# A hybrid trunk layer on one core: w_mod loads over all blocks of stage one, split low words in its last block, and blocks of 2, 3, 4, 4, 4 tiles in stage two

## The chip, the cores and the metric

The kernel runs on one core of one Trainium2 chip. The metric is the time of one execution on the device in microseconds, the median of several runs. The engines are named as in the profile: PE (TensorE matmul) and PEld (its weight loads), DVE (VectorE), ACT (ScalarE), POOL (GpSimd), SP (SyncE, which only issues DMAs here).

## The reference

One streaming step of one layer. The prompt is 2048 tokens of width 1024, and there are 8 samples of 16 tokens, with their own conditioning vectors, state and caches. All in float32:

```python
sh1, sc1, g1, sh2, sc2, g2 = split(silu(c) @ w_mod + b_mod, 6)      # w_mod 1024 x 6144
h = rmsnorm(x, norm1_g) * (1 + sc1) + sh1
proj = h @ w_in                                                     # 1024 x 3592
o_a = gated_delta(conv_silu(proj[q,k,v of A]), gate, beta, g)       # 4 heads x 128, state over time
o_b = band_attention(rmsnorm(q_b), rmsnorm(k_b), v_b, rel_bias)     # 8 heads x 64, own chunk of 64 and 8 before
x = x + g1 * (concat(o_a, o_b) @ w_out)
h = rmsnorm(x, norm2_g) * (1 + sc2) + sh2
x = x + g2 * (relu(h @ w_up) ** 2 @ w_down)                         # 1024 x 4096 x 1024
```

The outputs are y of prompt and samples, and the new convolution rows, delta states, and band keys and values.

## The kernel before

Tokens are cut into tiles of 128: tiles 0 to 15 are the prompt, tile 16 (SMP) holds the eight samples. To keep float32 precision every operand of a large product is a high word plus a low word, and each product is three matmuls (high x high, high x low, low x high; `mm3`, and lines 518 to 520 and 1477 to 1479).

`weights` brings one weight tile of 128 x 1024 words: the raw floats by DMA (line 174), the high word by a ScalarE copy (line 175), and the low word in one of two ways. The first time it is the difference raw minus high on GpSimd (line 82, called from line 180), and for chosen matrices it is stored to DRAM (line 183); later blocks load the stored word by DMA (line 178). w_in's low words are stored in the first block of stage one, those of w_out and w_down in the first block of stage two, those of w_up in its second. There are 3 buffers for raw and 4 for the split pair.

Stage one (`phase1`) goes over the blocks of tiles in BLOCKS1. Each block has a first projection (`proj_a`: gates, then 12 column tiles of q, k and v of the delta rule, `psq`, then gates again) and a second (`proj_b`: q, k and v of the attention, 12 weight tiles, `psb`). The second projections of the fifth and the third block (LATE, which counts from 0) come at the end, behind that of the last block. The last block has two tiles. The delta rule of a block runs as a generator beside the projections of the next one, and the attention of the first block of stage two beside the last three second projections.

w_mod has 48 pieces of 512 x 256. The 16 for sh1 and sc1 are loaded at the start; the other 32 wait in `mod_todo`. After each column tile of `proj_a` in a later block `mod_step` issues one (line 281, into a buffer of the tag x, of which there are three, shared with the rows of x), and two ticks later `mod_chunk` multiplies it, adds it to a row, and after each second piece finishes 256 columns of one section.

Stage two (`phase2`) goes over BLOCKS2. For each block it runs `out_proj` (`pso`) and then `ffn`: 32 columns of w_up (`psu`), and after each four of them two halves of w_down for each tile (`psd`). The attention of the *next* block is queued as a generator and its steps are spread over this `ffn` by `pace`, (8 + 1) steps for each tile and 4 more; where the next block holds SMP, the attention of the samples (`sample_gen`, 74 steps) follows in the same queue. A unit of attention is one head and one tile: scores (`psS`), softmax, transposes of the probabilities (`psP`), values (`pv`, line 1283, one matmul for each key tile: t + 1 for tile t, at most five). The `out_proj` of a block needs all units of its tiles. In the first block of stage two all low words are made on GpSimd, in the second those of w_up. When a block has four tiles, the first column of w_up is run in two parts of 256 tokens.

The order of the instructions on each engine is set when the program is built, by a scheduler with a timeline of its own; it can place an instruction of the next step ahead of one of the present step.

Of the kernel before, what the change touches and what calls it, by code (L numbers as in the profile page):

```python
# [8 lines left out]
F32 = mybir.dt.float32  # L9
# [5 lines left out]
P = 128  # L15
# [4 lines left out]
SMP = 16  # L20
# [10 lines left out]
EPS = 1e-6  # L31
NEG = -1.0e30
BLOCKS1 = [[0, 1, SMP], [2, 3, 4], [5, 6, 7], [8, 9, 10], [11, 12, 13], [14, 15]]
BLOCKS2 = [[0, 1], [2, 3, 4, 5], [6, 7, 8, 9], [10, 11, 12, 13], [14, 15, SMP]]
NGRP = 4
NT2 = max(len(b) for b in BLOCKS2)
LATE = (4, 2)
# [14 lines left out]
class Trunk:  # L52
# [113 lines left out]
    def weights(self, name, k0, c0, a, b):  # L166

        nc = self.nc
        n = a * b
        w = self.wp.tile([P, 2, 1056], F32R, tag="w", name="w", bufs=self.nw)  # L170
        v = lambda k: w[:, k, 0:n].rearrange("p (a b) -> p a b", a=a)
        src = self.i[name][0][k0 * P:(k0 + a) * P, c0:c0 + b].rearrange("(k p) c -> p k c", p=P)
        r = self.wp.tile([P, 1056], F32, tag="raw", name="raw", bufs=self.nraw)[:, 0:n]
        nc.sync.dma_start(r.rearrange("p (a b) -> p a b", a=a), src)
        nc.scalar.copy(w[:, 0, 0:n], r)  # L175
        key, kept = (name, k0, c0), self.s_w[name]
        if key in self.stored:
            nc.sync.dma_start(w.bitcast(F32)[:, 1, 0:n], kept[self.stored[key]][:, 0:n])
            return v(0), v(1)
        self.tt(w[:, 1, 0:n], r, w[:, 0, 0:n].bitcast(F32), ALU.subtract, eng=nc.gpsimd)  # L180
        if self.keep[name]:
            m = sum(k[0] == name for k in self.stored)
            nc.sync.dma_start(kept[m][:, 0:n], w.bitcast(F32)[:, 1, 0:n])
            self.stored[key] = m
        return v(0), v(1)
# [282 lines left out]
    def proj_a(self, tiles, hT, nxt=()):  # L468

        nc = self.nc  # L470
        n = len(tiles)
        T = n * P
        smp = SMP in tiles
        Tp = T - (P if smp else 0)
        blk = {}
        blk["kq"] = []
        ssq = self.bp.tile([P, self.nt, AH], F32, tag="ssq", name="ssq", bufs=2)
        ssk = self.bp.tile([P, self.nt, AH], F32, tag="ssk", name="ssk", bufs=2)
        ba = self.bp.tile([P, self.nt, 8], F32, tag="ba", name="ba", bufs=2)

        def gates(half):

            xs = [] if half else [self.normed(None, t) for t in nxt]
            m = 256 + 8 * half
            ws = self.wslices("w_in", 0, GA0 + 256 * half, m, KT, 4)
            for j, tl in enumerate(tiles):
                tmps = self.load_a(nxt[j], xs[j], 0, 1) if j < len(xs) else None
                ps = self.gp.tile([P, 512], F32, tag="g", name="psg")
                for k in range(KT):
                    wh, wl = ws[k]  # L490
                    self.mm3(ps[:, 0:m], hT[:, k, 0, j * P:(j + 1) * P], hT[:, k, 1, j * P:(j + 1) * P], wh, wl,
                             k == 0, k == KT - 1)
                th = self.cp.tile([P, 256], F32, tag="th", name="th", bufs=1)
                sg = self.cp.tile([P, 256], F32, tag="sgw", name="sgw", bufs=2)
                self.act(th, ps[:, 0:256], AF.Tanh, scale=0.5)
                self.stt(sg, th, 1.0, ps[:, 0:256], ALU.add, ALU.mult)
                if half:
                    nc.scalar.copy(ba[:, j], ps[:, 256:264])  # L498
                nc.sync.dma_start(self.s_sg[tl][:, half * 256:(half + 1) * 256], sg)
                self.tick(24 * 256)  # L500
                if tmps:
                    self.load_b(j, tmps)
            for j in range(len(tiles), len(xs)):
                self.load_b(j, self.load_a(nxt[j], xs[j], 0, 1))

        gates(1)
        for h in range(AH):
            kq = self.bp.tile([P, 2, self.nt * P], F32, tag="kq", name="kq", bufs=8)
            blk["kq"].append(kq)
            for sec in (1, 0, 2):  # L510
                c = sec * 4 + h
                ws = self.wslices("w_in", 0, c * P, P, KT, KT)
                ps = self.gp.tile([P, 512], F32, tag="g", name="psq")
                pc = ps[:, 4:4 + T]
                for k in range(KT):
                    wh, wl = ws[k]
                    mm = nc.tensor.matmul
                    mm(pc, wh, hT[:, k, 0, 0:T], start=(k == 0), stop=False)  # L518
                    mm(pc, wh, hT[:, k, 1, 0:T], start=False, stop=False)  # L519
                    mm(pc, wl, hT[:, k, 0, 0:T], start=False, stop=(k == KT - 1))  # L520
                self.tick(24 * T)
                dst = kq[:, 1 - sec] if sec < 2 else self.cp.tile([P, self.nt * P], F32, tag="vT", name="vT", bufs=2)
                y = self.cp.tile([P, self.nt * P], F32, tag="y", name="y", bufs=2)
                if Tp:
                    nc.scalar.copy(ps[:, 1:4], self.hist[:, c])
                    self.conv(y[:, 0:Tp], ps[:, 1:4 + Tp], c, Tp)
                    nc.scalar.copy(self.hist[:, c], ps[:, Tp + 1:Tp + 4])
                if smp:
                    pres = self.cp.tile([P, NB, 3 + SL], F32, tag="pres", name="pres", bufs=2)
                    hs = self.hists[:, c].rearrange("p (b w) -> p b w", w=3)  # L530
                    pv = pc[:, Tp:T].rearrange("p (b s) -> p b s", s=SL)
                    nc.scalar.copy(pres[:, :, 0:3], hs)
                    nc.scalar.copy(pres[:, :, 3:], pv)
                    nc.scalar.copy(hs, pv[:, :, SL - 3:])
                    self.conv(y[:, Tp:T].rearrange("p (b s) -> p b s", s=SL), pres, c, P, sub=True)
                self.act(ps[:, 0:T], y[:, 0:T], AF.Tanh)
                self.stt(dst[:, 0:T], ps[:, 0:T], 1.0, y[:, 0:T], ALU.add, ALU.mult)
                self.later(lambda c=c, dst=dst: self.qkv_out(c, dst, tiles, ssq, ssk))
                if self.bi:
                    self.mod_step()  # L540
        self.flush()
        gates(0)
        blk.update(ssq=ssq, ssk=ssk, ba=ba)
        return blk
# [481 lines left out]
    def phase1(self):  # L1026
        nc, tc = self.nc, self.tc
        with ExitStack() as st:
# [25 lines left out]
            last = len(B) - 1  # L1054
            self.load_hT(B[0], xs, 0, 1)
            for bi, tiles in enumerate(B):
                self.bi = bi
                self.keep["w_in"] = bi == 0
                if bi == 1:
                    self.rel_bias()  # L1060
                self.drain_to(bi - 2)
                blk = self.proj_a(tiles, self.hT, B[bi + 1] if bi in LATE else ())
                if bi == last:
                    break
                self.gdn(blk, tiles, bi)
                self.pace(0.95 * (cb(bi) * (bi not in LATE) + ca(bi + 1)), 6000)
                if bi not in LATE:
                    self.proj_b(tiles, self.hT, B[bi + 1])
# [3 lines left out]
            self.ap = R_("p1at")  # L1072
            self.queue(self.attention_first(BLOCKS2[0]), 1 + BH + BH // 2 * len(BLOCKS2[0]) + BH + 2, lane=2)
            self.queue(self.conv_gen(), 6, lane=1)
            self.gdn(blk, tiles, last)
            rest = [last] + list(LATE)
            self.pace(0.85 * sum(cb(b) for b in rest))
            for b, nb in zip(rest, rest[1:] + [None]):
                self.proj_b(B[b], self.hT, B[nb] if nb is not None else ())
            self.drain()  # L1080
            nc.sync.dma_start(self.o["gdn_prompt"][0, 0].rearrange("h k v -> k h v"), self.S)
# [242 lines left out]
    def sample_gen(self):  # L1324
# [7 lines left out]
        nc.sync.dma_start(bias, self.s_bs.rearrange("h s c -> (h s) c"))  # L1332
        nats = []
        for src in (self.s_q[SMP], self.s_kn):
            nat = self.sp.tile([P, 512], F32, tag="kn", name="nat", bufs=2)
            nc.sync.dma_start(nat, src)
            nats.append(nat)
        nc.vector.memset(qb, 0.0)
# [14 lines left out]
        for b in range(NB):  # L1353
# [4 lines left out]
            for t in range(4):  # L1358
                if t == 2:
                    yield  # L1360
                kn = self.sp.tile([P, 4, P], F32, tag="kn", name="kn", bufs=2)
# [163 lines left out]
    def phase2(self):  # L1525
        nc, tc = self.nc, self.tc
        with ExitStack() as st:
# [4 lines left out]
            self.hT = self.p2.tile([P, KT, 2, self.nt * P], F32R, name="hT2")  # L1532
            for bi, tiles in enumerate(BLOCKS2):
                n = len(tiles)
# [12 lines left out]
    def run(self):  # L1547
        self.nraw, self.nw = 3, 4
        self.deferred, self.lanes, self.pending, self.fill_rate, self.fill_acc = [], ([], [], []), [0, 0, 0], 0.0, 0.0
        self.front, self.solved, self.spent = 0, 0, 0  # L1550
        self.constants()
        self.phase1()
        self.phase2()
# [35 lines left out]
```

## Time and profile before

| | |
|---|---|
| median of 3 runs | 3214.93 us (3213.71 to 3215.14) |
| profiled execution | 3219.78 us |
| its span, first to last instruction | 3217.7 us |
| granted clock, mean | 0.975 |
| PE busy | 3072.2 us (95%) |
| DVE, ACT, POOL busy | 1765.4, 1471.7, 574.9 us |
| bytes moved by DMA | 751.62 MB |
| stage one ends, stage two begins | at about 1118 us |

A row of windows gives a stretch (start:end in us from the span's start), its length, then for PE, PEld, DVE, ACT and POOL the busy time and in brackets the number of instructions, then the granted TensorE clock as a share of full speed, the busy share of the 16 DMA engines, and GB/s. A row of waits gives who waited for whom, the total in us, how often, and the longest. A row of a group of instructions gives line, engine, operation, result and operands, shapes and count, then busy time and mean ns of one, then the idle time of the engine before them.

### The profile page before, as it was taken

How to read it: one execution, taken by the hardware profiler on the slowest of the kernel's cores; microseconds unless marked ns; L12 is line 12 of the kernel's file. 1: busy time of each engine (PE TensorE's matmuls, PEld its weight loads, DVE VectorE, ACT ScalarE, POOL GpSimd, SP SyncE). 2: the span in 40 equal slices, each digit the busy share in tenths (PEclk: the TensorE clock that was granted, in tenths of full speed). 3: DMA queues.
4: the chain of work that ended last, by engine and by line, in shares of the span. 5: the costliest groups of instructions: out<-in, count | busy, mean ns of one | idle time of the engine just before them, and what ended most of it. 6: DMA issues, size and time to landing. Idle time of an engine off the chain costs nothing.

```text
span 3217.7 us, 52979 instructions
## 1 busy us (share of the span) xinstructions
PE 3072.2 (95%) x19577; PEld 2720.7 (85%) x19577; DVE 1765.4 (55%) x4358; ACT 1471.7 (46%) x2803; POOL 574.9 (18%) x487
## 2 busy tenths in 40 slices
PE   6999999999989979988999999999999999998998
PEld 5998988899988978878888888888888887787997
DVE  4775777777868663777225556244556433243223
ACT  3554544555656555654334435344434433333332
POOL 3631212120212337631122110000000000000000
PEclk9999999999989989989999999999999999999999
DMA  9799897887978768885565666566675666677776
GB/s 295 232 291 292 255 295 222 258 263 240 298 244 272 227 224 265 253 289 159 177 200 182 211 232 213 179 191 200 196 258 176 213 226 225 221 245 227 255 247 196
DMA packets 630267, 751.62 MB, mean 234 GB/s; under 512 B 59808, under 2 KB 483728, under 8 KB 627960
## 3 DMA queue, kind: packets, MB, share of 16 engines
q1 hardware_dynamic: 624248, 716.78, 70.1%
q0 software_dynamic: 5760, 31.46, 2.9%
q8 instruction: 154, 2.52, 0.3%
q14 instruction: 105, 0.86, 0.1%
HBM read 635.48 MB, written 115.52 MB: 233 GB/s over the span
## 4 chain that ended last, share of the span: by engine, by line
PE 74%; DMA 14%; DVE 7%; ACT 2%; issue 2%; SPq 1%; POOL 1%; ACTq 0%; DVEq 0%; POOLq 0%
PE psu L1477 8%; PE psu L1478 7%; PE psu L1479 7%; PE psd L164 7%; PE psd L162 7%; PE psd L163 7%; PE psq L518 2%; PE psq L519 2%; PE psq L520 2%; PE psb L163 2%; PE psb L162 2%; PE psb L164 2%; PE pv L1283 2%; DMA x<-in_x_prompt_dram 2%; PE psS L1265 2%
## 5 line engine op out<-in xcount | busy, mean ns | idle before, releaser
L175 ACT CAST w<-raw 128x1024 fp32r<-128x1024 f32 (+1 forms) x528 | 551.8, 1047 | 359.2 <-PE psd L164 170.5
L1477 PE MATMUL psu<-hT,w 128*128 128x512 f32 (+2 forms) x1304 | 469.0, 361 | 4.2 <-ACT hT L104 4.2
L1478 PE MATMUL psu<-hT,w 128*128 128x512 f32 (+2 forms) x1304 | 468.3, 359 | 0.1
L1479 PE MATMUL psu<-hT,w 128*128 128x512 f32 (+2 forms) x1304 | 465.9, 357 | 0.3 <-POOL w L82 0.3
L162 PE MATMUL psd<-w,u 128*128 128x512 f32 x1088 | 431.0, 396 | 1.3 <-DVE u L82 0.8
L164 PE MATMUL psd<-w,u 128*128 128x512 f32 x1088 | 429.4, 396 | 0.0
L163 PE MATMUL psd<-w,u 128*128 128x512 f32 x1088 | 426.4, 392 | 0.0
L82 POOL TENSOR_TENSOR w<-raw,w 128x1024 fp32r<-128x1024 f32 (+1 forms) x132 | 320.1, 2434 | 325.0 <-ACT w L175 242.2
L79 DVE SCALAR_TENSOR_TENSOR psu<-psu,r 128x512 f32<-128x512 f32 (+2 forms) x160 | 98.9, 618 | 421.5 <-ACT r L92 421.4
L82 DVE TENSOR_TENSOR y<-y,psd 128x512 f32<-128x512 f32 x238 | 162.5, 685 | 246.2 <-PE psd L164 245.2
L1477 PEld LDWEIGHTS psu<-hT,w 128*128 128x128 f32 x1304 | 246.4, 189 | 38.1 <-ACT hT L104 4.9
L1479 PEld LDWEIGHTS psu<-hT,w 128*128 128x128 f32 x1304 | 246.4, 189 | 33.9 <-POOL w L82 0.9
L1478 PEld LDWEIGHTS psu<-hT,w 128*128 128x128 f32 x1304 | 246.5, 189 | 31.4 <-DVE hT L82 0.8
L92 ACT ACTIVATE r<-psu 128x512 f32<-128x512 f32 (+2 forms) x160 | 85.5, 534 | 380.0 <-issue 216.8
L164 PEld LDWEIGHTS psd<-w,u 128*128 128x128 f32 x1088 | 204.1, 188 | 46.5 <-DVE u L82 0.2
L163 PEld LDWEIGHTS psd<-w,u 128*128 128x128 f32 x1088 | 204.6, 188 | 45.6 <-issue 1.9
L162 PEld LDWEIGHTS psd<-w,u 128*128 128x128 f32 x1088 | 204.4, 188 | 44.6 <-DVE u L82 1.0
L162 PE MATMUL psb<-w,hT 128*128 128x256 f32 x816 | 237.5, 292 | 0.5 <-ACT hT L104 0.5
L163 PE MATMUL psb<-w,hT 128*128 128x256 f32 x816 | 235.4, 289 | 2.7 <-DMA w<-s_w_in 2.5
L164 PE MATMUL psb<-w,hT 128*128 128x256 f32 x816 | 235.1, 289 | 1.3 <-DVE hT L82 1.1
L518 PE MATMUL psq<-hT,w 128*128 128x384 f32 (+1 forms) x576 | 196.3, 341 | 8.3 <-ACT ba L498 8.2
L519 PE MATMUL psq<-hT,w 128*128 128x384 f32 (+1 forms) x576 | 194.7, 338 | 0.0
(316 smaller groups left out, 6501.2 us busy)
## 6 DMA issues: line engine op xcount, KB each, us to landing
raw<-in_w_up_dram SPq DMA_DIRECT2D x160, 512.0 KB
raw<-in_w_down_dram SPq DMA_DIRECT2D x160, 512.0 KB
raw<-in_w_in_dram SPq DMA_DIRECT2D x156, 512.0 KB
w<-s_w_in SPq DMA_DIRECT2D x130, 512.0 KB
w<-s_w_down SPq DMA_DIRECT2D x128, 512.0 KB
w<-s_w_up SPq DMA_DIRECT2D x96, 512.0 KB
raw<-in_w_out_dram SPq DMA_DIRECT2D x40, 512.0 KB
x<-in_x_prompt_dram SPq DMA_DIRECT2D x38, 512.0 KB
```

Of the source, the lines that this page charges most:

```text
L79: (eng or self.nc.vector).scalar_tensor_tensor(out, in0, scalar, in1, op0, op1)
L82: (eng or self.nc.vector).tensor_tensor(out, in0, in1, op)
L92: self.nc.scalar.activation(out, in_, func, **kw)
L162: mm(out, lh, rh, start=first, stop=False)
L163: mm(out, lh, rl, start=False, stop=False)
L164: mm(out, ll, rh, start=False, stop=last)
L175: nc.scalar.copy(w[:, 0, 0:n], r)
L518: mm(pc, wh, hT[:, k, 0, 0:T], start=(k == 0), stop=False)
L519: mm(pc, wh, hT[:, k, 1, 0:T], start=False, stop=False)
L1477: mm(ps[:, c0:c1], wh, h2[:, k, 0, c0:c1], start=(k == 0), stop=False)
L1478: mm(ps[:, c0:c1], wh, h2[:, k, 1, c0:c1], start=False, stop=False)
L1479: mm(ps[:, c0:c1], wl, h2[:, k, 0, c0:c1], start=False, stop=(k == KT - 1))
```

## The change

- BLOCKS2 becomes 2, 3, 4, 4 and 4 tiles; SMP stays in the last block, which now has three prompt tiles beside it.
- A counter `slot` runs over the 60 column tiles of the five later blocks of stage one; a piece of w_mod is loaded after 32 of them, evenly, and no longer after each of the first 32.
- A flag `mix` is set during both projections of the last block of stage one. While it is set, every other call of `weights` makes the low word on GpSimd although a stored one exists. It isn't stored again.
- In `sample_gen` the two tiles `nat` take buffers of the tag htmp and no longer those of kn.

```diff
-BLOCKS2 = [[0, 1], [2, 3, 4, 5], [6, 7, 8, 9], [10, 11, 12, 13], [14, 15, SMP]]
+BLOCKS2 = [[0, 1], [2, 3, 4], [5, 6, 7, 8], [9, 10, 11, 12], [13, 14, 15, SMP]]
...
         key, kept = (name, k0, c0), self.s_w[name]
-        if key in self.stored:
+        self.turn += self.mix
+        if key in self.stored and not (self.mix and self.turn % 2):
             nc.sync.dma_start(w.bitcast(F32)[:, 1, 0:n], kept[self.stored[key]][:, 0:n])
             return v(0), v(1)
         self.tt(w[:, 1, 0:n], r, w[:, 0, 0:n].bitcast(F32), ALU.subtract, eng=nc.gpsimd)
-        if self.keep[name]:
+        if self.keep[name] and key not in self.stored:
...
                 self.later(lambda c=c, dst=dst: self.qkv_out(c, dst, tiles, ssq, ssk))
-                if self.bi:
+                self.slot += self.bi > 0
+                if self.bi and self.slot * 32 // 60 > (self.slot - 1) * 32 // 60:
                     self.mod_step()
...
                 self.drain_to(bi - 2)
+                self.mix = bi == last
                 blk = self.proj_a(tiles, self.hT, B[bi + 1] if bi in LATE else ())
...
             for b, nb in zip(rest, rest[1:] + [None]):
+                self.mix = b == last
                 self.proj_b(B[b], self.hT, B[nb] if nb is not None else ())
...
         for src in (self.s_q[SMP], self.s_kn):
-            nat = self.sp.tile([P, 512], F32, tag="kn", name="nat", bufs=2)
+            nat = self.hp.tile([P, 4, P], F32, tag="htmp", name="nat", bufs=2).rearrange("p a b -> p (a b)")
             nc.sync.dma_start(nat, src)
...
+        self.slot, self.mix, self.turn = 0, False, 0
```

## Rows read from the trace of the kernel before

**Rows 1.** Windows of stage two: out-projection and feed-forward of blocks 1, 2, 4, 5.

```profile
1118.20:1162.00 43.80, 34.93 (x230) 33.09 (x231) 23.67 (x45) 16.66 (x29) 17.89 (x12) 0.81 0.99 341
1162.00:1413.90 251.90, 234.74 (x1520) 211.17 (x1520) 166.08 (x337) 148.83 (x274) 156.80 (x85) 0.97 0.77 243
1413.90:1503.00 89.10, 74.97 (x541) 71.68 (x540) 63.26 (x151) 38.55 (x73) 10.70 (x13) 0.85 0.59 193
1503.00:1920.70 417.70, 412.34 (x1999) 343.30 (x1997) 189.10 (x373) 172.73 (x286) 77.93 (x52) 0.99 0.60 197
1920.70:1975.40 54.70, 51.51 (x436) 50.93 (x434) 36.46 (x85) 20.06 (x34) 1.94 (x3) 1.00 0.68 236
...
2451.40:2885.90 434.50, 428.92 (x2411) 346.44 (x2410) 166.15 (x368) 170.60 (x276) 4.83 (x14) 0.99 0.68 220
2885.90:2930.60 44.70, 38.85 (x299) 38.10 (x298) 20.12 (x44) 10.42 (x13) 1.39 (x2) 0.92 0.88 273
2930.60:3217.70 287.10, 272.86 (x1361) 246.43 (x1358) 81.89 (x133) 97.72 (x141) 0.55 (x1) 0.98 0.72 228
```

**Rows 2.** Waits of PE from 1118 to 1503 us.

```profile
PE psP L1273 <- DVE sS L87: 10.3, 5, 5.6
...
PE psu L1479 <- POOL w L82: 0.3, 2, 0.2
```

**Rows 3.** Value matmuls of the first two attentions: ns min/median/max, first and last start.

```profile
L1283 PE MATMUL pv<-PT,KV x136: 274/282/582, 1158.3 to 1431.6; 128*128 128x256 f32 x136
...
L1283 PE MATMUL pv<-PT,KV x160: 274/281/415, 1449.9 to 1906.1; 128*128 128x256 f32 x160
```

**Rows 4.** Groups of VectorE's instructions by shape, 1195 to 1414 us.

```profile
L82 DVE TENSOR_TENSOR of<-otmp 64x128 f32<-64x128 f32 x20 | 22.7, 1133 | 1.1 <-DMA s_ob<-of 0.9
...
L87 DVE TENSOR_SCALAR sS<-sS,sm 128x640 f32<-128x640 f32 x10 | 12.5, 1252 | 0.3
```

**Rows 5.** The same groups, 2000 to 2390 us.

```profile
L87 DVE TENSOR_SCALAR sS<-sS,sm 128x640 f32<-128x640 f32 x24 | 13.2, 552 | 0.7
...
L82 DVE TENSOR_TENSOR of<-otmp 64x128 f32<-64x128 f32 x28 | 7.8, 280 | 0.4
```

**Rows 6.** Windows of stage one, second to sixth block; last row: sixth block's `proj_b`.

```profile
205.00:299.00 94.00, 92.62 (x689) 82.58 (x687) 56.37 (x151) 47.13 (x110) 2.98 (x5) 0.98 0.95 296
299.00:389.00 90.00, 86.85 (x733) 83.79 (x732) 58.86 (x166) 45.82 (x96) 29.89 (x28) 0.98 0.82 259
389.00:473.00 84.00, 80.94 (x498) 71.54 (x497) 67.87 (x181) 38.14 (x88) 12.80 (x11) 0.98 1.00 308
473.00:531.00 58.00, 53.66 (x521) 47.63 (x521) 41.72 (x117) 28.17 (x66) 13.40 (x13) 0.94 0.67 204
531.00:604.00 73.00, 72.93 (x463) 64.42 (x462) 59.75 (x188) 35.30 (x80) 8.12 (x10) 1.00 0.89 270
...
708.00:778.00 70.00, 69.00 (x487) 65.44 (x486) 52.67 (x165) 40.77 (x96) 3.20 (x4) 1.00 0.91 271
...
808.00:872.00 64.00, 60.31 (x496) 58.73 (x495) 55.63 (x191) 39.09 (x100) 12.42 (x11) 1.00 0.93 298
872.00:945.00 73.00, 65.52 (x559) 60.98 (x558) 40.53 (x139) 39.62 (x87) 12.79 (x19) 0.85 0.94 300
```

**Rows 7.** Timeline of PE: two starts, six matmuls of 256 columns apart.

```profile
910.20 0.28 PE L162 MATMUL psb<-w,hT 128*128 128x256 f32 x1
...
910.91 0.28 PE L162 MATMUL psb<-w,hT 128*128 128x256 f32 x1
```

**Rows 8.** Waits of PE from 2886 us to the end.

```profile
PE psh L345 <- DVE xn L87: 8.3, 2, 4.7
```

**Rows 9.** Issues of the later w_mod loads: ns min/median/max, first and last start.

```profile
L281 SPq DMA_DIRECT2D rawx<-in_w_mod_dram x32: 368/384/1625, 202.0 to 587.3; - x32
```

**Rows 10.** Waits of PE from 389 to 531 us.

```profile
PE ptq L552 <- DVE kq L79: 3.1, 1, 3.1
```

**Rows 11.** GpSimd's split of a weight tile, 1162 to 1414 us.

```profile
L82 POOL TENSOR_TENSOR w<-raw,w 128x1024 fp32r<-128x1024 f32 x63 | 151.8, 2416 | 68.6 <-ACT w L175 46.3 <-PE psu L1479 11.9 <-DMA raw<-in_w_up_dram 6.4
```

**Rows 12.** Waits of GpSimd from 808 to 945 us.

```profile
POOL KV L1136 <- PE pv L1180: 23.2, 2, 16.9
```

## The prediction, made before the changed kernel was run

> **What bounds the kernel now.** I read the windows of stage two first [rows 1], cut where the out-projection of a block ends and its feed-forward part begins. TensorE is busy nearly all the time, so the question is only where it is not, or not at full clock. For each window I use one number, called its loss: its length less PE's busy time, plus (1 - granted clock) times its length, since a matmul takes twice as long at the lower level. Idle time at the low level is counted twice, so it is an upper bound. In order, the losses of stage two are 17.2 us (8.9 + 8.3) for the first block's out-projection, 24.7 for its feed-forward, 27.5 (14.1 + 13.4) for the second's out-projection, and then 9.5, 3.2, 9.9, 9.4 and 20.0 (this last with the tail, where the output is written). The first block and its hand-over hold 69.4 us; nothing later is like it.
>
> Why there? The waits of PE in that stretch are led by the transposes of the probabilities, which wait for VectorE's softmax [rows 2]. The first block's feed-forward, of two tiles, carries the attention of four. Its value matmuls run until 1431.6 us, 17.7 us after the feed-forward ended (1413.9); those of the next block end at 1906.1, 14.6 us before theirs does [rows 3]. From its first to its last unit (32 units of head and tile), the first attention took 273 us, 8.8 us for each of 31 steps. It was going flat out and still came late, and the out-projection behind it had to wait. VectorE's share there also grew in size: with GpSimd busy 157 of 252 us, the sum of the two halves of a unit's output takes 1133 ns and the 640-wide softmax scaling 1252 ns [rows 4]; with GpSimd nearly idle they take 280 and 552 [rows 5].
>
> In stage one [rows 6] the losses are 3.3, 5.0, 4.7 and 7.8 us from 205 to 531 us (20.8 together), near nothing until 808, then 3.7 and 18.4 (7.5 idle, the rest clock 0.85) for 872 to 945 us, the last block's second projection. There the DMA engines are busy 0.94 of the time.
>
> **Part by part.**
>
> *Blocks of 2, 3, 4, 4, 4 for 2, 4, 4, 4, 3.* The sizes are the same set, so matmuls of the projections, and loads of weights, keep their number. Attention moves: the first feed-forward carries tiles 2 to 4, 24 units for 32, the second 32 units over three tiles for 32 over four, the fourth three tiles and the sample for two and the sample. Each moved five-wide unit is 3200 matmul columns; at 0.118 us for 256 [rows 7] 1.48 us, eight of them 12 us, off one block and onto another: zero in the sum, if PE has them ready.
> First block: its feed-forward has 234.7 us of PE work, now 223. With the end of the out-projection and about 20 us of loss, 24 units have some 247 us, 10.3 us each, against the 8.8 that were reached. So the late end goes. The hand-over's 27.5 then falls to about the 9.4 of the last out-projection, which has three tiles and no late attention: -18. Of the 41.9 ahead of it I take another -4: one q load in four and a quarter of the softmaxes are gone (a quarter is 10.5), but the start of the attention remains. -22; bounds -8 (late end shortened only) and -32.
> Second block: three tiles of feed-forward are 273 us of PE (the last window of [rows 1]), 32 units 47, an out-projection 45: 365 us, 11.4 us for a unit. That lies above 8.8 and under the 14.7 that the second attention had (456 us for 31 steps [rows 3]), and GpSimd splits only w_up there (78 us busy). So it should keep up; denser work costs a little: +4, bounds 0 and +39 (the losses of the first block's feed-forward and hand-over, 52.2, in place of 9.5 and 3.2). DMA: the storing of w_up's low words goes along into the shorter block. 197 GB/s over 418 us are 82 MB; over 335 us that is 245 GB/s, what the first feed-forward moves now (243, at a share of 0.77 [rows 1]) with 0.3 us of waits of PE for a weight split there [rows 2]. Zero.
> Last block: at its start PE waits 8.3 us for VectorE's normalised rows [rows 8]; with four tiles the first weight column runs in two parts, so that the first half begins earlier. A three-tile block without this now stands second. Gain and loss cancel: 0, bounds 6 either way. The fourth block gets one more tile of attention beside the sample; its loss of 9.9 over 434 us says there is room. Zero.
>
> *w_mod loads spread.* 32 loads of 0.5 MB, now one after each of the 32 first column tiles of blocks two to four (12, 12, 8), all between 202 and 587 us [rows 9]. After: 6, 6, 7, 6, 7 over five blocks. So six of them, 3.1 MB, leave the second and the third block each, where DMA is busy 0.95 and 1.00; each takes its four small matmuls, its addition and its part of the row with it. But no row has PE wait for one: from 389 to 531 us the largest wait is for VectorE (3.1 us [rows 10]). Work moves and does not vanish; of 20.8 I take -3, bounds -10 and +4 (4 us is what three more x tiles, waiting for the shared buffers in the fifth block, could cost: that block's loss is now near 0).
>
> *Every other weight tile splits its low word in the last block.* 14 of 28 loads of 0.5 MB go, 8 in the first projection (which gets 7 w_mod loads, 3.7 MB against 4.2 saved: even), 6 in the second. There a weight tile feeds two tiles, 24 matmuls, 2.8 us, and wants 1.05 MB: 370 GB/s, where 300 are moved at a share of 0.94. That window is bound by DMA; 3.1 MB less at 300 GB/s are 10.5 us. In exchange, a split of 2.42 us on GpSimd [rows 11] behind ScalarE's copy, on an engine busy 13 of 73 us. Cover: four weight buffers, three tiles ahead, 8.5 us. -9; bounds -15 and +10.
> Against it speaks that two VectorE instructions grew by 0.85 and 0.70 us where GpSimd was busy with such splits [rows 4, 5]. VectorE is busy 40.5 of 73 us in this window [rows 6], which covers 14 times 0.85, 12 us, over the last block; without the cover it is rival (b). The Trainium skill (SBUF — State Buffer, Who interferes with whom) has a rule that goes further: GpSimd's ports are VectorE's second pair, and a VectorE instruction that needs this pair, for a second SBUF input or a two-port mode, is shut out for the whole of a GpSimd instruction. The trace agrees in direction, with means grown by 0.85 and 0.70 us. By the rule, 14 splits of 2.42 us could hold VectorE for 34 us, an estimate from that page and the split's row, and the sum would be +13 with all of it on the path.
>
> *The rest.* The sample's two q and k tiles take the buffers of the transposed input, free in mid feed-forward; hidden behind PE at 98.7% busy in that block [rows 1], and 2 us if not. The extra condition on storing is never reached with storing on. Zero.
>
> Sum: -22 + 4 + 0 - 3 - 9 = -30. The profiled execution took 3219.78 us (span 3217.7, 2.1 around it): 3189.8. The median of the runs, 3214.93, is 4.85 lower; on that footing 3185.
>
> **Rivals.**
> (a) The attention has a rate, not a number: a unit needs about what it is given wherever VectorE, ScalarE and PE alternate. Then block one keeps its losses but for 8 us, and block two, more densely packed than now, comes late: +39 in its feed-forward and the next out-projection. -8 + 39 - 3 - 9 = +19: 3234. For it: the late end, and that units took 14.7 us in the second block; against: these were paced, and 8.8 was reached. It decides if a unit takes more than 11.4 us there.
> (b) GpSimd holds the split words back. It works in order, and in the last block it stood 16.9 us before a K and V load that waited for value matmuls [rows 12]. A split behind that is late by 16.9 less 8.5 of cover, 8.4 us, with the low clock after it +10: 3204. It needs the split to stand behind the load in the order. In its other form the 12 us of lengthened VectorE instructions lie on the path and nothing is gained: -22 + 4 - 3 + 12 = -9, 3206.
> (c) The late end goes only in part and the start of the attention costs as before: -8 for -22: 3199.
> (d) The change doesn't do what it says for time: spread loads meet no wait, half the low words are off a queue that is then waited for by others, and what block one gains block two loses: 3215.
>
> **Chances.** Forecast 0.54; (a) 0.11; (b) 0.13; (c) 0.12; (d) 0.10. A measurement of this kernel can tell about 0.2%, 6.4 us. Faster: forecast, (b) and (c), 0.79; same: (d), 0.10; slower: (a), 0.11. The forecast's own range is 3165 to 3202. All good bounds at once would be 3152; I reach to 3155, and up past (d) to 3218, leaving out (a) and little more.
>
> **What would show it.** Right: the value matmuls of the first attention end before the first down projection does; the second out-projection at a clock above 0.95 and under 60 us; the window of the last block's second projection some 9 us shorter with DMA share down and 6 splits on GpSimd; losses of the second feed-forward under 15. Wrong: value matmuls after the end of the second feed-forward (a), PE waiting for a w that GpSimd wrote in the last block (b), an unchanged first feed-forward (c). What would make it wrong in size is mostly the start of the attention, in the first out-projection and just behind it, which I left almost as it is, and the order of the instructions, which is fixed when the program is built and can shift anywhere.

## The result

| kernel | median, us | runs | to the kernel before |
|---|---|---|---|
| before, in the same set | 3213.76 (3209.55 to 3215.14) | 5 | 1 |
| changed | 3192.74 (3188.05 to 3202.53) | 5 | 0.9928 [0.9907, 0.9949] |
| changed, second set | 3197.25 (3184.76 to 3206.42) | 7 | 0.9948 [0.9928, 0.9967] |

By the ratio on record the change makes the kernel faster by 0.72%, 23 us of 3214, where 30 were forecast; the two medians of the table lie 21 us apart. In the second set it is 0.52%, 17 us. Gains and losses in us below are worked out from the ratios where no profile is named. The profiled execution of the changed kernel was the longest of its five: 3202.53 us, span 3200.8.

Windows of stage two of the changed kernel, with the columns of [rows 1]: out-projection and feed-forward of blocks one and two, the out-projection of block three, and both of block five.

```profile
1126.30:1168.10 41.80, 34.54 (x241) 32.18 (x242) 24.62 (x57) 18.71 (x35) 16.51 (x13) 0.88 1.02 352
1168.10:1407.60 239.50, 222.04 (x1430) 199.62 (x1428) 143.83 (x288) 137.92 (x248) 160.32 (x87) 0.96 0.82 254
1407.60:1461.00 53.40, 48.14 (x398) 46.98 (x396) 42.09 (x104) 27.33 (x49) 6.51 (x7) 1.00 0.76 258
1461.00:1792.30 331.30, 322.42 (x1771) 295.02 (x1770) 174.16 (x352) 163.47 (x281) 79.24 (x53) 0.99 0.77 251
1792.30:1847.60 55.30, 54.93 (x464) 54.52 (x463) 39.33 (x96) 22.38 (x39) 2.52 (x5) 1.00 0.67 230
...
2774.30:2829.30 55.00, 51.01 (x402) 49.74 (x401) 32.23 (x68) 12.89 (x19) 1.93 (x3) 0.94 0.73 231
2829.30:3200.80 371.50, 358.15 (x1578) 292.41 (x1576) 101.48 (x148) 105.64 (x143) 0.55 (x1) 0.99 0.58 181
```

By the prediction's measure (length less PE's busy time, plus one less the clock times the length) the first three rows lose 12.3, 27.0 and 5.3 us, 44.6 for the 69.4 of [rows 1]. The hand-over is what went: the second out-projection lost 27.5 at a clock of 0.85 and loses 5.3 at 1.00. The start of the attention stayed: the first two rows lose 39.3 us for 41.9, and the first feed-forward even 2.3 more than before. Block five, the last two rows, loses 24.4 us for 29.4.

The value matmuls of the first attention, of the first three units of the second (five matmuls each) at the hand-over, and of the rest of the second attention, in the form of [rows 3]:

```profile
L1287 PE MATMUL pv<-PT,KV x96: 274/282/580, 1150.3 to 1400.2; 128*128 128x256 f32 x96
...
L1287 PE MATMUL pv<-PT,KV x15: 277/281/290, 1430.5 to 1436.2; 128*128 128x256 f32 x15
...
L1287 PE MATMUL pv<-PT,KV x145: 274/282/562, 1455.4 to 1783.6; 128*128 128x256 f32 x145
```

The first attention ends at 1400.2, 7.4 us before the next out-projection begins (1407.6); before, it ended 17.7 us after. The second, from 1430.5 to 1783.6 over 31 steps, took 11.4 us for a unit, the number that the prediction worked out for it, and ends 8.7 us before its out-projection.

Windows of stage one of the changed kernel: the second block, and the last block's first and second projection.

```profile
206.00:299.00 93.00, 90.95 (x682) 82.52 (x681) 60.01 (x167) 50.83 (x116) 8.27 (x8) 0.98 0.93 283
...
804.00:883.00 79.00, 71.59 (x584) 64.30 (x583) 71.62 (x202) 40.12 (x103) 31.21 (x22) 1.00 0.79 237
883.00:936.00 53.00, 48.15 (x414) 44.83 (x411) 41.73 (x124) 31.60 (x65) 26.45 (x24) 0.94 0.89 271
```

The last row was 63.2 us long before (871.6 to 934.8, shown below; the 73 us of [rows 6] reach into the next projection): 10 us shorter, as costed. But the row above it has VectorE busy 71.62 of 79 us. For that row the prediction had put gain and loss as even.

At the end, PE's wait for the normalised rows of the last block, 8.3 us in [rows 8], in the same view of waits from 2774 us on:

```profile
PE psh L346 <- DVE xn L87: 1.4, 2, 1.0
```

### The profile page after: what moved, and what is told of

It is laid out like the page before. It is cut to its first block, busy times and chain, and to the rows that moved or that the text cites. A ratio compares the mean times of both kernels' runs of the same rounds, so it can differ in the third digit from the quotient of the medians.

```text
span 3200.8 us, 52974 instructions
## 1 busy us (share of the span) xinstructions
PE 3061.2 (96%) x19577; PEld 2714.0 (85%) x19577; DVE 1772.8 (55%) x4358; ACT 1473.2 (46%) x2803; POOL 607.6 (19%) x501
## 4 chain that ended last, share of the span: by engine, by line
PE 73%; DMA 11%; DVE 9%; ACT 3%; issue 2%; SPq 1%; POOL 1%; ACTq 0%; POOLq 0%; DVEq 0%
PE psu L1481 7%; PE psu L1483 7%; PE psu L1482 7%; PE psd L164 7%; PE psd L162 7%; PE psd L163 7%; PE psb L163 2%; PE psb L162 2%; PE psb L164 2%; PE psS L1269 2%; PE pso L162 2%; PE pv L1287 2%; PE pso L163 2%; PE pso L164 2%; PE psq L519 2%
## 5 line engine op out<-in xcount | busy, mean ns | idle before, releaser
L82 POOL TENSOR_TENSOR w<-raw,w 128x1024 fp32r<-128x1024 f32 (+1 forms) x146 | 352.7, 2425 | 279.6 <-ACT w L175 231.5
```

Source lines behind the costliest of these rows:

```text
L82: (eng or self.nc.vector).tensor_tensor(out, in0, in1, op)
```

## The experiments

Each ratio is to runs of the kernel before in the same set. To see where a part acts, I cut each profiled execution at four points of PE's timeline: the first `psb` of the second block (up to there it is 293 to 301 us in all of them, and left out), of the fourth block, of the last block, of the late blocks, and the first `pso`. "Solve" counts the `pw` and `kS` matmuls of the delta rule in the last block's second projection. Each row is one profiled execution: two kernels with the same stage one differ by up to 6 us in a stretch (314.4 and 320.2 for the splits alone and with the sizes).

| kernel | ratio [95%] | blocks 2 to 4 | 4 to last | last, 2nd proj. | late ones | stage two | solve |
|---|---|---|---|---|---|---|---|
| before | 1 | 315.1 | 257.6 | 63.1 | 183.4 | 2099.5 | 72, 0 |
| changed | 0.9928 [0.9907, 0.9949] | 307.0 | 277.1 | 53.1 | 190.3 | 2074.5 | 40, 0 |
| changed, second set | 0.9948 [0.9928, 0.9967] | 305.0 | 278.0 | 52.2 | 192.9 | 2073.6 | 40, 0 |
| sizes alone | 0.9947 [0.9930, 0.9964] | 313.8 | 260.2 | 59.7 | 183.2 | 2080.7 | 72, 0 |
| spread alone | 1.0072 [1.0054, 1.0089] | 305.9 | 275.4 | 85.4 | 168.3 | 2098.6 | 72, 16 |
| splits alone | 0.9997 [0.9981, 1.0013] | 314.4 | 271.3 | 49.7 | 182.5 | 2096.2 | 48, 0 |
| sizes, splits | 0.9955 [0.9938, 0.9973] | 320.2 | 272.5 | 50.3 | 181.6 | 2084.5 | 48, 0 |
| sizes, half of the splits | 0.9931 [0.9908, 0.9954] | 313.9 | 261.7 | 50.1 | 184.0 | 2080.2 | 48, 0 |
| the same, again | 0.9953 [0.9934, 0.9971] | 313.9 | 262.4 | 50.5 | 188.5 | 2086.2 | 48, 0 |
| spread, own buffer | 1.0062 [1.0041, 1.0083] | 302.6 | 278.1 | 79.8 | 176.4 | 2088.8 | 72, 16 |
| sizes, half, spread to four | 0.9943 [0.9921, 0.9964] | 298.7 | 283.2 | 51.1 | 189.3 | 2068.8 | 48, 0 |
| sizes 2, 4, 3, 4, 4 | 0.9999 [0.9985, 1.0014] | 316.9 | 257.7 | 59.3 | 184.6 | 2095.7 | 72, 0 |
| sizes, spread | 1.0018 [1.0003, 1.0033] | 306.9 | 280.0 | 85.4 | 166.6 | 2082.6 | 72, 16 |
| sizes, half, spread to five | 1.0017 [0.9997, 1.0037] | 301.8 | 276.9 | 82.4 | 173.1 | 2084.3 | 72, 16 |

**Sizes alone**, with the changed `nat` buffers. All edits here are to the changed kernel.

```diff
-                if self.bi and self.slot * 32 // 60 > (self.slot - 1) * 32 // 60:
+                if self.bi:
...
-                self.mix = bi == last
+                self.mix = False
...
-                self.mix = b == last
+                self.mix = False
```

> Only the block sizes of stage two (2, 3, 4, 4, 4) and the two sample tiles in other buffers; w_mod loads and the last block of stage one as before. Theory: the gain is all in stage two, where the changed kernel's profile is 25 us shorter (2074.5 against 2099.5) and stage one 8 us longer; so about 3213.8 - 25 = 3189, no slower than the whole change (3192.7). Rival: the parts in stage one gain too and only the one profiled execution hid it; then this alone stays at 3198 or above.

Measured: 0.9947, 17 us, between the theory and its rival. Its second out-projection, in the columns of [rows 1]:

```profile
1400.00:1453.00 53.00, 48.74 (x403) 47.55 (x402) 42.01 (x103) 27.84 (x49) 7.02 (x8) 1.00 0.76 260
```

It looks like that of the whole change. This part alone gives nearly all that the change gives.

**Spread alone and splits alone**: the kernel before with the condition on `slot`, and with the two lines that set `mix`.

> Only the 32 w_mod loads spread over five blocks. Theory: the late part of stage one, blocks five and six, becomes as tight on VectorE as blocks two and three were, and the last first projection waits for it; 0 to +8 us, 3214 to 3222. Rival: spreading relieves DMA and VectorE in blocks two and three, -3 us, 3211, and the loss in block six came from the splits on GpSimd.

> Only every other weight tile of stage one's last block split on GpSimd. Theory: it shortens the last block's second projection by what the changed kernel's profile shows in loss, 5 us (3209), and costs nothing in the first projection. Rival: the splits lengthen VectorE's instructions in the last first projection, which then loses 4 to 9 us, and the sum is zero or above, 3214 to 3218.

Measured: 1.0072, 23 us slower, which neither theory nor rival had, and 0.9997. So neither part does what its term said. For the splits, the table shows both halves: 49.7 for 63.1 in the second projection, but 271.3 for 257.6 ahead of it. Windows of the last block's two projections, before:

```profile
808.00:871.60 63.60, 59.91 (x492) 58.33 (x491) 55.30 (x190) 38.91 (x99) 12.02 (x11) 1.00 0.93 299
871.60:934.80 63.20, 55.72 (x510) 52.20 (x508) 35.88 (x126) 35.64 (x78) 12.45 (x17) 0.90 0.94 301
```

and with the splits alone:

```profile
801.00:879.10 78.10, 66.83 (x493) 62.88 (x492) 66.78 (x190) 40.09 (x101) 29.01 (x19) 0.93 0.68 200
879.10:928.80 49.70, 44.67 (x446) 42.77 (x444) 39.93 (x110) 30.99 (x67) 25.02 (x21) 1.00 0.88 272
```

In the first rows PE runs 492 and 493 matmuls and VectorE 190 instructions both times, but VectorE's busy time rises from 55.3 to 66.8 us, while the DMA share falls from 0.93 to 0.68. Groups of VectorE's instructions in that first projection (busy us, mean ns, idle before them), before:

```profile
L82 DVE TENSOR_TENSOR E<-E,incl 128x512 f32<-128x512 f32 x3 | 2.1, 685 | 0.9 <-POOL Ds L82 0.9
L79 DVE SCALAR_TENSOR_TENSOR z<-z,zs,sg 128x128 f32<-128x128 f32 x12 | 3.4, 345 | 0.1
L82 DVE TENSOR_TENSOR Ds<-Ds,ta 128x110 f32<-128x110 f32 x1 | 0.3, 274 | 0.0
```

and with the splits alone, with GpSimd's split of the same stretch in the last line:

```profile
L82 DVE TENSOR_TENSOR E<-E,incl 128x512 f32<-128x512 f32 x3 | 5.6, 1865 | 2.3 <-POOL Ds L82 2.3
L79 DVE SCALAR_TENSOR_TENSOR z<-z,zs,sg 128x128 f32<-128x128 f32 x12 | 5.5, 520 | 0.0
L82 DVE TENSOR_TENSOR Ds<-Ds,ta 128x110 f32<-128x110 f32 x1 | 2.4, 2436 | 0.0
...
L82 POOL TENSOR_TENSOR w<-raw,w 128x1024 fp32r<-128x1024 f32 x7 | 16.7, 2386 | 24.6 <-ACT w L175 24.6
```

A subtraction that took 274 ns takes 2436, the length of one split. The timelines of GpSimd and VectorE show it beside its split:

```profile
867.53 2.38 POOL L82 TENSOR_TENSOR w<-raw,w 128x1024 fp32r<-128x1024 f32 x1 [10.09 <-ACT w L175]
...
867.60 2.44 DVE L82 TENSOR_TENSOR Ds<-Ds,ta 128x110 f32<-128x110 f32 x1
```

Six of the seven splits in this stretch stand so beside one VectorE instruction, which begins 0.07 to 0.88 us after the split and ends 0.02 to 0.55 us behind it. Together these six take 13.8 us; at the mean times of such instructions before they are 2.5. That is 11.4 us, all of VectorE's growth. VectorE was busy 87% of this stretch (55.3 of 63.6) and had no room for it. In none of the profiles with splits does a wait of PE in the last block name a word that GpSimd had still to write.

**Sizes and splits, without the spread.**

> The change without the spread loads: block sizes and splits, w_mod loads after each of the first 32 column tiles as before. Theory: the spread costs and the splits gain, so this beats the whole change: 3189 - 5 = 3184. Rival: the spread gains 3 us, so this is slower than the whole change, 3195.

Measured: 0.9955, the sizes alone within the spread of the runs. The theory, 3184 us, fell. The first projection's loss (272.5 for 260.2) and the second's gain (50.3 for 59.7) cancel again.

**Splits in the second projection alone**, with the sizes and the w_mod loads as before, run in two sets.

```diff
-                if self.bi and self.slot * 32 // 60 > (self.slot - 1) * 32 // 60:
+                if self.bi:
...
-                self.mix = bi == last
+                self.mix = False
```

> Block sizes, and splits on GpSimd only in the last block's second projection (six tiles); its first projection loads all low words again; w_mod loads as before. Theory: the splits cost in the first projection, because VectorE is the bound there (55.6 of 64 us busy before) and each split holds one of its instructions for up to 2.4 us, and gain some 10 us in the second, which DMA bounds. So this gains 8 to 12 us on block sizes alone (ratio 0.9947): about 0.991, 3184. Rival: what the splits cost and gain is the order of instructions as built, not VectorE; then this is like block sizes with all splits, 0.9955, or like block sizes alone.

> Block sizes and splits only in the last block's second projection, a second time and on the same chip as the changed kernel itself: which of the two is the better version. Theory: its stage one is 10 us or more shorter than the changed kernel's, ratio 0.991 to 0.993 and 5 to 10 us below it. Rival: within the spread of runs the two are equal.

Measured: 0.9931 and 0.9953. The last block's second projection keeps its 50 us and the stretch ahead of it costs 261.7 and 262.4, not 272. With the late projections, which take up to 5 us more, this half gives 4 to 9 us in the profiles (234.1 and 239.0 for 242.9). The times, on both sides of the 0.9947 of the sizes alone, can't tell such a gain, and 0.991 was not reached.

**The spread with a buffer of its own**, added to the spread alone, because the x rows of a block and the pieces share three buffers.

```diff
-            rv = self.mod_load(*c, self.hp.tile([P, D], F32, tag="x", name="rawx", bufs=self.nx))
+            rv = self.mod_load(*c, self.cp.tile([P, D], F32, tag="xm", name="rawx", bufs=1))
```

> As the spread loads alone (ratio 1.0072), but the w_mod pieces get one buffer of their own and no longer take the three that the rows of x use. Theory: the loss of the spread is that the rows of x for the fifth block's second projection can't be loaded 80 us ahead, at 792 us, but only from 878 us on, in the stretch that DMA bounds; with a buffer of their own they come early, the stop between the last block's second projection and the next one's (31 us in the spread alone, 9 before) shrinks to about 10, and the ratio is 0.998 to 1.001. Rival: it is the 3.7 MB of w_mod in the last block themselves, or what its additions cost VectorE; then the stop stays above 20 us and the ratio above 1.004.

Measured: 1.0062 for 1.0072. The stop between the two projections is still 21.5 us long (31.3 in the spread alone), above the 20 that the rival named. The buffer isn't the main cause; that theory fell.

**Spread over four blocks**, none of it in the last, with the sizes and half of the splits.

```diff
-                if self.bi and self.slot * 32 // 60 > (self.slot - 1) * 32 // 60:
+                if self.bi and self.slot * 32 // 48 > (self.slot - 1) * 32 // 48:
```

> As block sizes with splits in the second projection only, and the w_mod loads spread over four blocks (8 each), none in the last. Theory: without loads in the last block the rows of x are loaded early again, and blocks two and three are relieved by 4 each: equal to the same kernel without the spread or up to 5 us faster, 0.989 to 0.991. Rival: the spread costs wherever it lies beside the reloaded blocks, here in the fifth: 0.993 or above.

Measured: 0.9943, as the rival had it. The last block's second projection is back at 51.1 us. What blocks two to four give (298.7 for 313.9) the next ones take (283.2 for 262).

**Sizes 2, 4, 3, 4, 4**, which leave the first hand-over as it was.

> Only block sizes, but 2, 4, 3, 4, 4: the first block's feed-forward carries four tiles of attention again, and the last block still has four tiles. Theory: the gain of the sizes lies in the hand-over from the first to the second block, so it goes: value matmuls end after the first feed-forward, the second out-projection has 20 us or more of loss again, ratio 0.997 to 1.001. Rival: the gain lies in ending on a full block; ratio about 0.995 as with 2, 3, 4, 4, 4.

Measured: 0.9999. Windows of the first feed-forward and the second out-projection, and the value matmuls of the first attention:

```profile
1158.00:1409.00 251.00, 233.15 (x1518) 209.76 (x1516) 165.16 (x337) 148.77 (x274) 156.30 (x85) 0.97 0.78 244
1409.00:1493.00 84.00, 70.67 (x526) 68.41 (x525) 59.58 (x145) 36.26 (x68) 9.80 (x12) 0.88 0.61 199
...
L1287 PE MATMUL pv<-PT,KV x136: 274/282/562, 1154.1 to 1426.0; 128*128 128x256 f32 x136
```

The attention of four tiles is back in a feed-forward of two, ends 17 us late, the out-projection behind it takes 84 us at a clock of 0.88, and the gain is gone, as the theory said. The last block has four tiles here too, so ending on a full block isn't what gains.

**The changed kernel again, and sizes with the spread but no splits.**

> The changed kernel itself once more, since its profiled execution (3202.5 us) was the slowest of its five runs (median 3192.7). Theory: its first stage costs some 5 to 10 us over that of before in any execution, and the median of 3192.7 is the block sizes (-18) with run to run spread; so ratio about 0.994 to 0.996, stage two beginning at 1120 us or later. Rival: the profiled execution was unlucky in stage one; then stage two begins before 1115 us and the ratio stays at 0.993 or below.

> Block sizes and spread loads, no splits on GpSimd in the last block. Theory: the 3.7 MB of w_mod in the last block lie in a stretch bound by DMA, and only the splits make room for them; without splits the block sizes' -0.5% are given back and more: 0.9947 + 0.0065 = 1.001, with the last block's second projection (to the start of the next one) at 75 us or more. Rival: the loss of the spread alone was one order of instructions as built; then this stays near 0.995.

Measured: 0.9948 and 1.0018. Both theories held (stage two of the changed kernel begins at 1128 us). So the spread costs 23 us beside the sizes too (1.0018 for 0.9947), and next to nothing when all splits are there.

**Which half of the splits pays for the spread?** The whole change with the splits in the second projection alone.

> The changed kernel with its split words kept to the second projection of stage one's last block (all loads of stored words in the first). It asks which half of the splits pays for the spread w_mod pieces. Theory: the pieces' price lies in the second projection, which DMA bounds; there the splits take 3.1 MB away, so it is at 50 to 54 us as in the changed kernel (85 with the spread and no splits), and the first projection, free of the 12 us that VectorE was held for, costs no more than with the spread alone. Then some 10 us less than the changed kernel: 3183 to 3188, ratio to the kernel before 0.990 to 0.992. Rival: in the first projection of the last block too it is the bytes, seven pieces or 3.7 MB more against 4.2 MB that splits would save; without those splits the first projection loses what VectorE gains, and the time is that of the changed kernel or up to 10 us more: 3195 to 3207, ratio 0.994 to 0.998. If the second projection stays near 80 us and the ratio is at 1.000, the second half of the splits is not what pays.

Measured: 1.0017. The theory's number for the second projection failed: it takes 82.4 us with half of its stored words gone, the sign that the expectation named for the second half not being what pays. So the first half pays: alone it costs 12 us, beside the spread it is worth 22 to 29 (0.9948 and 0.9928 for 1.0017). Windows of it, whole and in tens:

```profile
877.70:960.00 82.30, 76.44 (x608) 68.17 (x607) 51.70 (x157) 40.77 (x88) 28.67 (x27) 0.81 0.77 235
...
890.00:900.00 10.00, 8.72 (x76) 7.97 (x75) 9.22 (x26) 4.37 (x9) 7.71 (x7) 1.00 0.95 277
900.00:910.00 10.00, 6.95 (x61) 5.91 (x60) 9.03 (x21) 5.54 (x10) 5.52 (x6) 0.89 0.46 103
910.00:920.00 10.00, 10.00 (x79) 8.70 (x77) 3.33 (x11) 3.59 (x9) 2.94 (x5) 0.60 1.10 350
920.00:930.00 10.00, 10.00 (x84) 8.64 (x83) 2.49 (x8) 3.22 (x6) 2.36 (x1) 0.57 0.40 126
930.00:940.00 10.00, 10.00 (x61) 8.80 (x61) 3.24 (x14) 5.30 (x14) 1.01 (x1) 0.50 0.88 278
```

Bytes don't bind it as a whole: the DMA engines are busy 0.77 of the time. From 900 to 910 us PE has work for 7 of 10 us, and from then to 940 it runs at 0.60, 0.57 and 0.50, the lower of its two levels at the end. Its longest waits from 893 to 915 us say for whom it had stood still, and the timelines say why:

```profile
PE ptT L789 <- DVE TW L790: 3.1, 2, 2.6
...
903.58 2.35 POOL L82 TENSOR_TENSOR w<-raw,w 128x1024 fp32r<-128x1024 f32 x1
...
903.58 2.63 DVE L82 TENSOR_TENSOR qraw<-qraw,qkg 128x256 f32<-128x256 f32 x1
906.14 0.27 DVE L790 COPY TW<-ptT 32x128 f32<-32x128 f32 x1
...
906.46 0.30 PE L789 MATMUL ptT<-ident,A 32*32 32x32 f32 x8 [2.60 <-DVE TW L790]
```

The matmul is part of the solve of the delta rule, in which PE and VectorE take turns. The copy that it needs stood on VectorE behind a product (`qraw`) that took 2.63 us beside a split of this very projection; the one ahead of it, of the same shape, took 0.42. So here a split brought the wait. Groups of PE's matmuls in this projection:

```profile
L796 PE MATMUL pw<-TW,A 32*32 32x32 f32 (+1 forms) x72 | 6.2, 242 | 0.0
...
L820 PE MATMUL kS<-S,kq 128*128 128x128 f32 x16 | 2.7, 281 | 0.0
```

The whole change has 40 of the first and none of the second here (the last column of the table). The kernels with the spread to five blocks and without the first projection's splits all have 72 and 16, and all take 80 to 85 us for this projection. Two of them, the spread alone and the sizes with the spread:

```profile
880.20:965.60 85.40, 74.94 (x640) 68.13 (x639) 51.12 (x175) 43.50 (x95) 19.79 (x25) 0.87 0.90 296
```

```profile
883.20:968.60 85.40, 76.27 (x640) 69.78 (x638) 51.36 (x175) 43.10 (x95) 19.98 (x25) 0.86 0.91 295
```

These two have no splits. PE's longest single wait in both, 2.4 us, is for a ScalarE copy (`qraw`), their low clock lies in several short pieces, and the `psb` of the last block end at 934 and 936 us, 31 and 33 us before the next projection's: in between PE works mostly at the delta rule. So the three have the length in common, but not one cause.

By the prediction's measure these three lose 21.5, 21.6 and 21.1 us, against 13.8 before, 8.0 in the changed kernel and 4.3 with the sizes and half of the splits.

## Why the prediction was right, and where it was not

**The sizes: right, in mechanism and size.** The term was -22 for the first block with its hand-over, +4 for the second, 0 for the rest: -18. Shown: the sizes alone give 17 us, the stretch from the first `pso` on falls from 2095.8 us (mean of the four profiles that keep the old sizes) to 2079.5 (mean of nine with the new ones), and sizes that keep the late attention give nothing. Within it the losses of the first block and the hand-over fell by 24.8, and those of the second feed-forward and the out-projection behind it are 12.6 for 12.7. Block five, put at 0 with bounds of 6, gave 5.0. Rival (a) fell: the second attention went at 11.4 us a unit and was in time. So did the price of (c), as the late end went wholly; its second half, that the start of the attention costs as before, nearly came true (39.3 us for 41.9).

**The splits in the second projection: 4 to 9 us for 9 in the profiles, too little for the times to show.** The stretch is 10 us shorter and the DMA share falls from 0.97 to 0.89 (sizes alone, and sizes with half of the splits, below). Part of this is delta-rule work that now runs later (48 `pw` matmuls for 72), which is why the late projections give some of it back. GpSimd did stand before a K and V load, as rival (b) in its first form wanted (7.4 us with the sizes and half of the splits), but no wait of PE for a word from GpSimd followed. Some of these splits hold a VectorE instruction too, but VectorE was busy 36 of 60 us: here there was cover.

```profile
870.10:929.80 59.70, 54.93 (x510) 51.64 (x508) 36.23 (x126) 35.24 (x78) 12.44 (x17) 0.91 0.97 316
```

```profile
870.20:920.30 50.10, 45.77 (x455) 43.32 (x453) 38.96 (x110) 32.08 (x69) 24.78 (x21) 1.00 0.89 275
```

**The splits in the first projection: the step that failed first.** The prediction put this half at "even", by bytes (4.2 MB saved, 3.7 MB added), and named VectorE's room in the second projection only (40.5 of 73 us) as the cover for the whole block. In the first projection VectorE was busy 87% of the time; the cover wasn't there. The half costs 12 us (271.9 for 259.9, means of the profiles with and without it), which is rival (b) in its second form, confined to this projection. That the size agrees is luck: the prediction had 14 splits at a mean of 0.85 us, the trace has six that held VectorE for 1.9 us each. The rule of the Trainium skill (SBUF — State Buffer, Who interferes with whom), that a VectorE instruction with two SBUF inputs contends with a GpSimd instruction that reads SBUF, and that the later of the two is blocked for the whole of the first, is borne out by the 2436 ns above.

**The spread of the w_mod loads: the term that was wrong in sign.** -3 was taken, with +4 as the upper bound; it costs 23 us, alone and beside the sizes. "Work moves and does not vanish" was right: the 32 later pieces with the finishing of their rows take PE 31.2 us before (21.5 and 9.65), so eleven of them 10.7, and blocks two to four become 10.6 us shorter (304.9 for 315.5, means of six and seven profiles). So only the work left these blocks; the 3 us of waits that the prediction took off didn't go. And the stretch from the fourth block to the last grows by 17.7 (277.6 for 259.9): the work, and some 7 us of waits and lower clock. In the last block more of the delta rule lands in the second projection, and with the late projections this takes 254.0 us for 244.4, +10, of which two pieces are 2 and most of the rest waits and low clock. No one cause of these waits is shown; in the profile where the longest is followed above, it was a split. These stretches make 17 of the 23 us. I had bounded the harm by three x tiles that wait for a buffer, and never asked what work the pieces would push behind them.

**The two parts don't add.** Spread and all splits together cost, beside the sizes alone, nothing that the runs can tell (0.9928 and 0.9948 for 0.9947), where their sum would be 26 us (+23 and +3). One place is shown: from the fourth block to the last the two cost 17.7 us together, as much as the spread does by itself, so that the splits' 12 us don't come on top. In the changed kernel the same stretch has only four splits that hold a VectorE instruction, for some 7 us. Behind it they add up: the splits give 10 us there (234.3 for 244.4, mean of four), the spread costs 10, and both together leave 244.2, and with the splits in the first projection more of the solve stays out of the second, which takes 53 us and not 85. That is 12 us of the 26; the two profiled executions of the changed kernel lie 10 and 6 us above the medians of their sets, which may hold some of what is left; that isn't shown. Why the order that is set when the program is built puts the solve there in the one case and not in the other wasn't settled.

So the sum of -30 came out at -23, and at -17 in the second set, where the sizes alone give -17: the terms of stage one, -12 together, came to -6 to 0. Behind the total stand a sound term of -18, one of -9 that the profiles bear out for one half of the splits, and two that were off by 12 and by 26 us when tried singly. That this one combination takes most of that back is luck; no step of the prediction had it. The sizes with half of the splits, and without the spread, reach the same time (0.9931 and 0.9953); no kernel here was shown to be faster than the changed one.

## What to carry to other kernels

Where a change moves elementwise work to another engine, take the cover from each stretch in which the work lies, by the engine that is busiest there: a price by bytes is no price where VectorE is at 87%. When pieces are moved to later blocks, cost what they push behind them. Try the parts of a change singly: here one of three carried all of the gain that the runs can tell, one came to nothing, and the third is harmless only beside the second.

## What the runs showed of the hardware

A 110-column VectorE subtraction took 2436 ns beside one of GpSimd's splits (2386 ns in the mean), and 274 ns without them: it was held for nearly a whole split, and ended 0.13 us behind it. Such a hold can reach PE: a 256-column product of VectorE that took 2.63 us beside a split made PE wait 2.6 us, with 7 us of work in 10, and 30 us at 0.60, 0.57 and 0.50 of the clock followed, although PE was busy all of that time.
